# A second up group of each feed-forward as seven block products, and the weave ratio at 0.68

## The chip, the cores and the metric

One core of one Trainium2 chip. The metric is device time in microseconds (us); three runs of the kernel before gave a median of 2243.52 us, from 2241.81 to 2245.09. The profiled execution took 2241.73 us, of which 2240.0 us are the span from the first to the last instruction.

## The reference

One decoder layer in float32 on 256 tokens of width 2048: a SwiGLU feed-forward, a mixer, and a second feed-forward of the same shape. The mixer is not touched here. Each feed-forward computes

```
h = (silu(x @ w_gate) * (x @ w_up)) @ w_down      # w_gate, w_up: 2048 x 5504; w_down: 5504 x 2048
x = x + 0.5 * rms_norm(h, g)
```

The left factor x has 256 rows, so it is two blocks of 128 tokens. All products are made to nearly float32 accuracy: every operand is split into a high and a low part, and three TensorE products stand for one (high by high, high by low, low by high).

## The kernel before, in words

**Names.** PE is TensorE, ACT ScalarE, DVE VectorE, POOL GpSimd. A weight tile of 128 x 1024 floats (512 KB) is loaded by SP's queue into one of 12 buffers `raw`; ACT copies its high part to `whi` (line 171), and DVE subtracts to get the low part `wlo` (line 172). This pair is called a split below. There are five `whi` and five `wlo` buffers, so ACT can make the split of a tile only when PE is done with the split five places earlier. Each engine carries out its instructions in its queue's order.

**Plain group.** `linear_steps` (line 287) multiplies both token blocks by a strip of weights: for each pair of 128-row slices of the weight one split, and 2 x 2 x 3 = 12 matmuls of 512 columns. A gate or up group of 1024 columns is two such strips with 16 slices each: 192 matmuls and 16 splits. Each batch is 12 matmuls, but the last of a strip is 24 with two splits, first 12 for token block 0, then 12 for block 1.

**Seven products.** `sevens` (line 394) makes a group of 1024 columns as a product of 2 x 2 blocks (two token blocks or column halves by two halves of the inner dimension) with seven block products instead of eight, on sums and differences of blocks. The forms of x are made once per feed-forward (`new_forms`). Each block product p has four units s = 0 to 3; a unit is one split and six matmuls, so a group has 28 units, 168 matmuls, 28 splits. Phase one has products 1 and 2 (8 units). Phase two has products 3, 5, 6, 7 and 4 (20 units), with the weights of 5, 6 and 7 summed by DVE in place in the raw tile (line 403, three a round), and the weight of product 4 completed by POOL: an accumulating DMA (line 459) adds a weight block from memory into the raw tile r[0], after product 6 has read that tile. The order of phase two is set by delays; at its end it is p3 s3, p5 s3, p4 s2, p6 s3, p7 s3, p4 s3. Seven DVE additions (lines 455 to 477) put the products together.

```
def t4(s, r):
    G.dma_start(out=r[0].rearrange("p (k c) -> p k c", c=512), in_=src(1, 0, s), accum_op=ALU.add)
    return r[0]
for p, ps in phase(8 * g + 4, [(3, 0, lambda s, r: r[2]), (5, 1.1, lambda s, r: add(r[0], r[1])),
                               (6, 2.2, lambda s, r: add(r[0], r[2])), (7, 3.3, lambda s, r: add(r[2], r[1])),
                               (4, 6.4, t4)]):
```

**Blocks.** `ffn` (line 593) goes by five blocks of 1024 columns (f = 0, 8, 16, 24, 32 in units of 128) and a rest of 384. The gate of block 0 is plain and runs ahead. The gates of f = 8, 16, 24, 32 and the up group of f = 32 are seven-product groups: five groups, 840 matmuls, called the side. The plain up groups of f = 0, 8, 16, 24 with the down products of those blocks (`down_steps`, 192 matmuls a block), and the rest's gate and up (96 matmuls of 384 columns each), are the main work: 1728 matmuls. The down products of the last block and the rest follow after.

**The weave.** `weave` (line 268) sets the order, and PE runs in it. After each batch of n main matmuls it gives the side n x RATIO of credit, and side units are put out while credit is above zero. Where the main work needs a side group (`yield "gate", f`), the missing units are put out one after another with nothing between.

```
credit += n * ratio
while side is not None and credit > 0:
    n = next(side, None)
```

**Up results.** In a plain up strip, `up` (line 624) multiplies the sum by the silu of the gate on DVE (line 627) for each token block, and the transposes of the result on PE (line 178) come after the next 12 matmuls. `up_seven` (line 664) does the multiplication for a whole group (line 668, four DVE instructions), and its transposes come with the main batch that follows.

Of the kernel before, what the change touches and what calls it, by code (L numbers as in the profile page):

```python
# [33 lines left out]
BIG = 5  # L34
BLOCK = 8
AHEAD = 3
UP_SEVEN = (4,)
RATIO = 0.5


def constants():
# [16 lines left out]
def layer(ctx: ExitStack, tc: tile.TileContext, a, out: bass.AP):  # L58
# [191 lines left out]
    def run_soon():  # L250
        while soon:
            soon.pop(0)()
# [15 lines left out]
    def weave(main, side, done, ratio):  # L268


        credit = 0.0
        for n in main:
            if not isinstance(n, int):
                while n not in done:
                    credit -= next(side)
                continue
# [3 lines that stand above are left out]
                if n is None:  # L280
                    side = None
                else:
                    credit -= n
        for _ in side or ():
            pass
# [307 lines left out]
    def ffn(u, r, first, then, head, wg, wu, wd, gpost, resid, keep, gname, final, unscale=None):  # L593
# [23 lines left out]
        def gate_seven(c, f):  # L617
            for t in range(2):
                for i in range(2):
                    x = c[t][:, i * 512:i * 512 + 512]  # L620
                    S.activation(x, x, AF.Silu, scale=scale(t, 1 if i == 0 else -1))
                sg[f][t] = c[t]
# [41 lines left out]
        def up_seven(c, f):  # L664
            for t in range(2):
                for i in range(2):
                    g = sg[f][t][:, i * 512:i * 512 + 512]
                    V.scalar_tensor_tensor(g, c[t][:, i * 512:i * 512 + 512], scale(t, 1 if i == 0 else -1), g, ALU.mult, ALU.mult)

            def later():  # L670
                for i in (0, 4):
                    hT[f + i] = (slot([P, 4, 2, P], F32R, "hh"), slot([P, 4, 2, P], F32R, "hl"))
                    hh, hl = hT[f + i]
                    for t in range(2):
                        split_T(hh[:, :, t, :], hl[:, :, t, :], sg[f][t][:, i * P:(i + 4) * P], 4)

            soon.append(later)
# [4 lines left out]
        for f in range(BLOCK, last, BLOCK):  # L682
            groups.append((("gate", f), wg, f * P, lambda c, f=f: gate_seven(c, f)))
            if f // BLOCK in UP_SEVEN:
                groups.append((("up", f), wu, f * P, lambda c, f=f: up_seven(c, f)))

        def main():
            for f in range(0, last, BLOCK):
                if f and f // BLOCK in UP_SEVEN:
                    if f < f0:  # L690
                        yield "up", f
                        run_soon()
                else:
                    if f:
                        yield "gate", f
                    yield from up_steps(f)
                if f < f0:
                    yield from down_steps(f)
            yield from linear_steps(lu, Weights(KD, chunks(wg, last, m)), lambda t, ps: gate_plain(t, ps, last))
            yield from linear_steps(lu, Weights(KD, chunks(wu, last, m)), lambda t, ps: up(t, ps[0], last, 0, m))  # L700

        done = set()
        weave(main(), sevens(forms, groups, done), done, RATIO)
        run_soon()
# [521 lines left out]
```

## Time and profile before

| | us |
|---|---|
| median of three runs | 2243.52 |
| profiled execution, whole | 2241.73 |
| its span | 2240.0 |
| PE busy | 2201.4 (98% of the span) |
| DVE busy | 1571.3 (70%) |
| ACT busy | 1223.3 (55%) |
| POOL busy | 138.5 (6%) |

The span is the time between the first and the last instruction. Busy time counts each engine's own instructions; a high share does not say that the engine never waits in a given stretch.

### The profile page before, as it was taken

The numbers are of one execution on the slowest core, as the hardware profiler recorded it, in microseconds if no ns is written. First come the engines' busy times: TensorE is split into PE (matmuls) and PEld (weight loads), VectorE is DVE, ScalarE is ACT, GpSimd is POOL, SyncE is SP. The second block draws the span as 40 slices with busy tenths as digits, with TensorE's granted clock in tenths as the row PEclk, the third lists the DMA queues.
The fourth block names the chain that finished last, engine by engine and source line by source line (L and its number), as shares of the span: only waits on it lengthen the run. The fifth ranks groups of instructions, "written<-read, shape, count | busy, mean of one in ns | idle before, by whom it ended". The sixth has DMA issues, their size and how long they took to land.

```text
span 2240.0 us, 28549 instructions
## 1 busy us (share of the span) xinstructions
PE 2201.4 (98%) x10434; PEld 1873.4 (84%) x10434; DVE 1571.3 (70%) x1859; ACT 1223.3 (55%) x1560; POOL 138.5 (6%) x177
## 2 busy tenths in 40 slices
PE   8999999999999999999999999999999999999997
PEld 6888888888887799999888888887888888887886
DVE  6787787877776758686655545558777777787866
ACT  7665656565554654545444444456655565655544
POOL 1001001010011000000000000000010010100110
PEclk9999999999999999999999999999999999999999
DMA  8578879797888464456655566755778797988981
GB/s 326 160 246 239 275 219 285 224 278 235 256 231 314 151 209 127 151 156 182 196 182 192 187 197 204 234 190 181 250 237 275 217 289 232 267 249 245 236 300 55
DMA packets 229245, 497.41 MB, mean 222 GB/s; under 512 B 18360, under 2 KB 51344, under 8 KB 229104
## 3 DMA queue, kind: packets, MB, share of 16 engines
q1 hardware_dynamic: 203456, 436.32, 59.0%
q0 software_dynamic: 25472, 59.20, 12.5%
q8 instruction: 81, 1.33, 0.2%
q14 instruction: 60, 0.49, 0.1%
q10 hardware_dynamic: 176, 0.07, 0.0%
HBM read 472.44 MB, written 23.07 MB: 221 GB/s over the span
## 4 chain that ended last, share of the span: by engine, by line
PE 48%; DVE 2%; issue 1%; DMA 1%; ACT 1%; DVEq 0%; POOL 0%; ACTq 0%; POOLq 0%
PE acc L322 13%; PE acc L319 13%; PE acc L320 13%; PE acc L443 3%; PE acc L441 3%; PE acc L442 3%; PE tp L178 1%; DMA raw<-in_ffn_wu_dram 1%; DVE wlo L172 1%; DMA raw<-in_ffn_wd_dram 0%; ACT whi L171 0%; DVE y L568 0%; DVE ym L568 0%; ACT junk L167 0%; ACT uh L189 0%
## 5 line engine op out<-in xcount | busy, mean ns | idle before, releaser
L172 DVE TENSOR_TENSOR wlo<-raw,whi 128x1024 fp32r<-128x1024 f32 (+2 forms) x937 | 1095.5, 1182 | 557.8 <-ACT whi L171 532.0
L171 ACT ACTIVATE whi<-raw 128x1024 fp32r<-128x1024 f32 (+2 forms) x937 | 953.8, 1028 | 786.8 <-PE acc L322 612.6
L319 PE MATMUL acc<-whi,uh 128*128 128x512 f32 (+1 forms) x1620 | 605.5, 374 | 0.0
L320 PE MATMUL acc<-wlo,uh 128*128 128x512 f32 (+1 forms) x1620 | 600.6, 371 | 4.0 <-DVE wlo L172 4.0
L322 PE MATMUL acc<-whi,ul 128*128 128x512 f32 (+1 forms) x1620 | 525.0, 371 | 0.0
L320 PEld LDWEIGHTS acc<-wlo,uh 128*128 128x128 f32 x1620 | 304.9, 188 | 47.1 <-DVE wlo L172 5.7
L319 PEld LDWEIGHTS acc<-whi,uh 128*128 128x128 f32 x1620 | 305.2, 188 | 41.8 <-ACT mv L796 0.3
L322 PEld LDWEIGHTS acc<-whi,ul 128*128 128x128 f32 x1620 | 302.0, 188 | 41.4
L319 PE MATMUL acc<-whi,hh 128*128 128x512 f32 x688 | 268.1, 390 | 0.0
L320 PE MATMUL acc<-wlo,hh 128*128 128x512 f32 x688 | 267.8, 389 | 0.0
L322 PE MATMUL acc<-whi,hl 128*128 128x512 f32 x688 | 259.4, 389 | 0.0
L320 PEld LDWEIGHTS acc<-wlo,hh 128*128 128x128 f32 x688 | 129.2, 188 | 26.8
L319 PEld LDWEIGHTS acc<-whi,hh 128*128 128x128 f32 x688 | 129.2, 188 | 26.8
L322 PEld LDWEIGHTS acc<-whi,hl 128*128 128x128 f32 x688 | 129.1, 188 | 26.8
L403 DVE TENSOR_TENSOR raw<-raw,raw 128x1024 f32<-128x1024 f32 x120 | 146.3, 1219 | 0.3
L441 PE MATMUL acc<-whi,sh 128*128 128x512 f32 x320 | 126.5, 395 | 0.0
L443 PE MATMUL acc<-whi,sl 128*128 128x512 f32 x320 | 125.0, 391 | 0.0
L442 PE MATMUL acc<-wlo,sh 128*128 128x512 f32 x320 | 124.8, 390 | 0.0
L441 PE MATMUL acc<-whi,uh 128*128 128x512 f32 x240 | 95.1, 396 | 3.7 <-ACT whi L171 3.7
L442 PE MATMUL acc<-wlo,uh 128*128 128x512 f32 x240 | 94.2, 393 | 1.2 <-DVE wlo L172 1.2
L443 PE MATMUL acc<-whi,ul 128*128 128x512 f32 x240 | 94.1, 392 | 0.0
L459 POOL DMA_DIRECT2D raw<-in_ffn_wg_dram x32 | 38.8, 1213 | 641.1 <-DVE wlo L172 523.3
(323 smaller groups left out, 1912.0 us busy)
## 6 DMA issues: line engine op xcount, KB each, us to landing
raw<-in_ffn_wg_dram SPq DMA_DIRECT2D x192, 512.0 KB, 5.0
raw<-in_ffn_wd_dram SPq DMA_DIRECT2D x172, 512.0 KB, 6.2
raw<-in_ffn_wu_dram SPq DMA_DIRECT2D x168, 512.0 KB, 5.2
raw<-in_w_gate_dram SPq DMA_DIRECT2D x96, 512.0 KB, 4.4
raw<-in_w_in_dram SPq DMA_DIRECT2D x192, 192.0 KB, 2.7
raw<-in_ffn_wg_dram POOLq DMA_DIRECT2D x32, 512.0 KB, 8.9
ysum<-part POOLq DMA_DIRECT2D x64, 256.0 KB, 6.5
raw<-in_w_o_dram SPq DMA_DIRECT2D x32, 512.0 KB, 4.6
```

The costliest lines, as they stand in the source:

```text
L171: S.activation(hi, src, AF.Copy)
L172: return V.tensor_tensor(lo, src, f32(hi), ALU.subtract)
L178: PE.transpose(p[:, i, :], src[:, i * P:(i + 1) * P], ident)
L319: PE.matmul(ps[t][c], lh, wh[:, sl], start=(k == 0), stop=False)
L320: PE.matmul(ps[t][c], lh, wl[:, sl], start=False, stop=False)
L322: PE.matmul(ps[t][c], ll, wh[:, span[c]], start=False, stop=(k == nk - 1))
L403: V.tensor_tensor(x, x, y, ALU.add)
L441: PE.matmul(bank[p], ah[:, k, :], hi[:, ws], start=(seen[p] == 0), stop=False)
L442: PE.matmul(bank[p], ah[:, k, :], lo[:, ws], start=False, stop=False)
L443: PE.matmul(bank[p], al[:, k, :], hi[:, ws], start=False, stop=(seen[p] == 7))
L459: G.dma_start(out=r[0].rearrange("p (k c) -> p k c", c=512), in_=src(1, 0, s), accum_op=ALU.add)
```

## The change

The up group of f = 16 (block 2 when the first is block 0) joins the side as a sixth seven-product group, between the gates of f = 16 and f = 24. Its plain up strips leave the main work, which now asks for the group itself (`yield "up", 16`) ahead of the down products of that block. The ratio goes from 0.5 to 0.68. Both feed-forwards use the same function, so both change.

```
-UP_SEVEN = (4,)
-RATIO = 0.5
+UP_SEVEN = (2, 4)
+RATIO = 0.68
```

The lines that read the two constants:

```
groups.append((("gate", f), wg, f * P, lambda c, f=f: gate_seven(c, f)))
if f // BLOCK in UP_SEVEN:
    groups.append((("up", f), wu, f * P, lambda c, f=f: up_seven(c, f)))
...
if f and f // BLOCK in UP_SEVEN:
    if f < f0:
        yield "up", f
        run_soon()
...
weave(main(), sevens(forms, groups, done), done, RATIO)
```

## Rows read from the trace of the kernel before

**Rows 1.** Engine share by stretch: both weaves (start:end, length, busy us, clock, DMA share, GB/s).
```profile
116.50:686.70 570.20, 567.92 (x2567) 473.66 (x2565) 433.09 (x400) 322.74 (x349) 53.67 (x60) 1.00 0.84 250
1578.00:2150.80 572.80, 567.99 (x2567) 473.67 (x2565) 435.33 (x401) 324.37 (x349) 53.79 (x60) 1.00 0.84 250
```

**Rows 2.** Timeline of PE, second feed-forward (start, duration, engine, line, instruction, idle before it).
```profile
1788.62 0.39 PE L441 MATMUL acc<-whi,sh 128*128 128x512 f32 x1
...
1791.34 0.39 PE L319 MATMUL acc<-whi,hh 128*128 128x512 f32 x1
...
2145.97 0.33 PE L319 MATMUL acc<-whi,uh 128*128 128x384 f32 x1
...
2147.89 0.34 PE L322 MATMUL acc<-whi,ul 128*128 128x384 f32 x1
```

**Rows 3.** Timeline of DVE, POOL, ACT, DVE and PE at the end of group gate 16.
```profile
1790.40 3.51 DVE L172 TENSOR_TENSOR wlo<-raw,whi 128x1024 fp32r<-128x1024 f32 x3 [0.57 <-ACT whi L171]
...
1793.06 1.20 POOL L459 DMA_DIRECT2D raw<-in_ffn_wg_dram  x1 [2.48 <-DVE wlo L172]
...
1801.74 2.01 ACT L171 ACTIVATE whi<-raw 128x1024 fp32r<-128x1024 f32 x2 [5.01 <-DMA raw<-in_ffn_wg_dram]
...
1802.84 1.23 DVE L172 TENSOR_TENSOR wlo<-raw,whi 128x1024 fp32r<-128x1024 f32 x1 [4.85 <-ACT whi L171]
...
1806.30 0.39 PE L441 MATMUL acc<-whi,uh 128*128 128x512 f32 x1
```

**Rows 4.** Timeline of POOL and ACT: the same at the first and the last such end.
```profile
215.33 1.24 POOL L459 DMA_DIRECT2D raw<-in_ffn_wg_dram  x1 [2.81 <-DVE wlo L172]
...
224.94 2.01 ACT L171 ACTIVATE whi<-raw 128x1024 fp32r<-128x1024 f32 x2 [5.94 <-DMA raw<-in_ffn_wg_dram]
...
2024.23 1.19 POOL L459 DMA_DIRECT2D raw<-in_ffn_wg_dram  x1 [18.80 <-DVE wlo L172]
...
2033.35 2.96 ACT L171 ACTIVATE whi<-raw 128x1024 fp32r<-128x1024 f32 x3 [5.23 <-DMA raw<-in_ffn_wg_dram]
```

**Rows 5.** Line 459 by itself: its accumulating transfers.
```profile
DMA to landing us min/median/max: 5.6/8.9/11.8
```

**Rows 6.** Timeline of PE at the end of the last side group, both feed-forwards.
```profile
686.74 0.50 PE L441 MATMUL acc<-whi,uh 128*128 128x512 f32 x1 [1.13 <-ACT whi L171]
688.00 0.50 PE L442 MATMUL acc<-wlo,uh 128*128 128x512 f32 x1 [0.76 <-DVE wlo L172]
...
2150.82 0.79 PE L441 MATMUL acc<-whi,uh 128*128 128x512 f32 x1 [2.60 <-ACT whi L171]
2152.08 0.79 PE L442 MATMUL acc<-wlo,uh 128*128 128x512 f32 x1 [0.47 <-DVE wlo L172]
```

**Rows 7.** Timeline of PE: stops for an up result, and one outside the weave.
```profile
576.11 0.66 PE L178 MATMUL tp<-ident,sg 128*128 128x128 f32 x4 [1.19 <-DVE sg L627]
...
696.00 1.53 PE L178 MATMUL tp<-ident,sg 128*128 128x128 f32 x12 [1.83 <-DVE sg L668]
...
770.93 0.70 PE L320 MATMUL acc<-wlo,uh 128*128 128x384 f32 x2 [3.51 <-DVE wlo L172]
...
2038.71 0.66 PE L178 MATMUL tp<-ident,sg 128*128 128x128 f32 x4 [2.23 <-DVE sg L627]
```

**Rows 8.** Engine share by stretch of 10 us (the number before the DMA share is the clock).
```profile
770.00:780.00 10.00, 8.87 (x46) 8.16 (x47) 9.79 (x26) 6.78 (x20) 2.16 (x4) 0.83 0.73 236
...
2030.00:2040.00 10.00, 7.77 (x37) 6.20 (x36) 5.56 (x7) 3.67 (x5) 0.00 (x0) 1.00 0.85 278
...
2150.00:2160.00 10.00, 8.71 (x32) 7.69 (x33) 9.20 (x13) 5.82 (x7) 1.59 (x3) 0.66 1.03 415
```

**Rows 9.** Groups of instructions by line (count, busy us, mean ns of one, idle before).
```profile
L172 DVE TENSOR_TENSOR wlo<-raw,whi 128x1024 fp32r<-128x1024 f32 (+2 forms) x937 | 1095.5, 1182 | 557.8 <-ACT whi L171 532.0
L171 ACT ACTIVATE whi<-raw 128x1024 fp32r<-128x1024 f32 (+2 forms) x937 | 953.8, 1028 | 786.8 <-PE acc L322 612.6
...
L403 DVE TENSOR_TENSOR raw<-raw,raw 128x1024 f32<-128x1024 f32 x120 | 146.3, 1219 | 0.3
...
L474 DVE TENSOR_TENSOR sg<-sg,acc 128x512 f32<-128x512 f32 x10 | 6.8, 680 | 0.0
```

## The prediction

> **What bounds the kernel now.** I read the engine shares over the two weaves first, then PE's timeline for the places where it stops, then the other engines just ahead of each stop. In each weave PE is busy 568 of 570 to 573 us [rows 1], so there every matmul costs its full distance to the next: twelve of 512 columns take 1791.34 - 1788.62 = 2.72 us, 0.227 us each; eleven steps of 384 columns take 1.92 us, 0.174 each [rows 2]. DVE is busy 433 us (76%) and ACT 323 (57%) [rows 1]. So the bound is PE, and the question is where PE will stop.
>
> The place that matters is the end of each side group. The last product-4 unit (p4 s3) needs a raw tile that POOL's accumulating transfer completes, and that transfer can only start when p6 s3, two side units earlier, has been split. At the end of gate 16 it goes out at 1793.06, ACT gets the tile at 1801.74 after 5.01 us of idling, the low half is there at 1802.84 + 1.23 = 1804.07, and PE wants it one matmul after 1806.30 [rows 3]: 2.5 us to spare. All later splits stand behind that one on ACT and DVE meanwhile. Of the eight ends of gate groups seven show this wait on ACT, with 8.1 to 9.9 us (mean 9.1) from issue to ACT's start; the first has 9.6 and the last 9.1 [rows 4].
>
> **The time PE must cover.** With five split buffers, p6 s3 can be split once PE has left the split five places before it. From there to p4 s3 PE has a fixed number of matmuls to run, counted from the loops. Before, the four gate groups of each feed-forward all end with 72 matmuls in that stretch, 72 x 0.227 = 16.3 us. At gate 16 the unit five places earlier is the one whose first matmul is the 1788.62 row [rows 2], so it ends 1.36 us later, at 1789.98. The need is thus 3.1 us to POOL's issue, 9.1 us on the way, and 1.06 + 1.2 us minus one matmul (2.0) for the two halves: 14.2 us, 13.3 to 15.0 by the shortest and longest way. It fits into 16.3.
>
> **The change, part by part (both feed-forwards alike).**
>
> *Matmuls removed.* 192 plain matmuls become 168: 24 fewer, 48 in the kernel, 48 x 0.227 = -10.9 us. The Trainium skill (TensorE: Matmul & The Clock Gate, "Wait — 56ns, not 53.3ns?") gives 215.7 ns for 512 columns at the full clock; by it this term would be -10.4 us; the row says 0.227, and I keep that.
>
> *Work added elsewhere.* 12 more splits (DVE 1.18 us, ACT 1.03), 12 additions of 1.22 and seven of 0.68 [rows 9]: DVE +14.2 + 14.6 + 4.8 = 33.6 us, so (433 + 34)/565 = 83% of the weave; ACT +12 and a copy, 60%. The up product's own DVE work and 16 transposes stay the same in number. Taken at nothing, because PE's matmuls cover it: the heaviest mix (phase two beside a plain up strip) keeps DVE at about 90%. If the cover fails, the price is rival 3. POOL issues four more accumulating transfers and SP four more loads (20 for 16), 4.2 MB per weave on about 143 MB (250 GB/s x 570 us), share 0.84 to about 0.87: nothing, unless the accumulates land later, which the upper end of the need holds. POOL's new transfers stand in its queue among the writes of block 8's down sums, each waiting for an ACT copy; a transfer of up 16 caught behind one has 2.1 us to spare there (16.3 against 14.2). The new loads stand in SP's queue among those of the main strips, which now come 12% slower (one batch and its credit: 20.2 matmuls against 18).
>
> *Ends of groups moved.* This is what the ratio does. At 0.5 one batch of 12 is followed by one unit; at 0.68 by one or two, so there is less main work between p6 s3 and p4 s3. Counting the loops again with six groups at 0.68 gives, for the same stretch:
> - gate 8: 54 matmuls, 12.2 us; short of 14.2 by 2.0 (1.1 to 2.8)
> - gate 16: 60, 13.6 us; short by 0.6 (0 to 1.4)
> - up 16: 72, 16.3 us; nothing
> - gate 24: 48, 10.9 us; short by 3.3 (2.4 to 4.1; nothing with the shortest row of line 459, rival 1). The main work reaches `yield "gate", 24` with 960 x 0.68 = 653 of the 672 matmuls it needs, so the last four units are put out back to back
> - gate 32: 78, 17.7 us; nothing
> - up 32, in the rest: before 24 x 0.227 + 48 x 0.174 = 13.8 us, and PE stopped there: 1.13 + 0.76 us of waits in the first and 2.60 + 0.47 in the second [rows 6]. Now 24 and 36: 11.7 us, so +2.1 on top of that stop.
>
> Sum: 2.0 + 0.6 + 3.3 + 2.1 = 8.0 per feed-forward, +16.0. A wait of PE is lost for good, since PE bounds both sides of it.
>
> *New place: the transposes of up 16.* Between the last matmul of up 16 and its transposes PE has 6 + 12 = 18 matmuls (4.1 us); ahead of them DVE has one addition and four multiplications, some splits between. The nearest row is the same step for up 32, 1.83 us of waiting [rows 7]; from none to 1.8, I take 1.0: +2.0 for both.
>
> *Stops that go.* Before, gate 32 ends in the last batch of a plain up strip, where DVE, held at the late tile, keeps the up multiplication waiting: 1.19 and 2.23 us [rows 7]. Now it ends in a down strip with 17.7 us. With the empty queue behind each, -3.7 us. What is late next there: nothing that these rows show.
>
> *The clock.* A stop of 2.60 us was followed by a stretch at 0.66 of full clock, one of 3.51 by 0.83; one of 2.23 kept 1.00 [rows 6 to 8], the levels being 2.4 and 1.2 GHz. At the lower level 10 us lost 3.4 and 1.7 us of full clock. The stop at gate 24 (two parts, about 2.3 and 1) lies at that border, that of up 32 in the first feed-forward (now about 3.2) beyond it. Zero to three drops; I take the middle, 1.5 x 2.55 = +3.8.
>
> Sum: -10.9 - 3.7 + 16.0 + 2.0 + 3.8 = +7.2. On the profiled 2241.73 us that is 2248.9. This execution lies 1.8 us below the median of 2243.52, against which the change will be timed: 2250.7 us.
>
> **Rivals.**
> 1. *The tile comes in time: faster.* If the transfer lands in 5.6 us, the shortest of line 459 [rows 5], the need falls from 14.2 to 10.7 us, under all gate groups' cover; it decides at about 7 us for gate 8 and 5.7 for gate 24. Left: -10.9 - 3.7 + 4.2 (up 32) + 2.0 = -8.4, 2235 us. For: the shortest row. Against: seven ends at 8.1 or more with DMA at 0.84. The compiler may also hoist p6 s3's split ahead of a main one, with the same effect. On the page's side: the Trainium skill (DMA: Bandwidth & Descriptors, "Anatomy of one DMA — SWDGE (gpsimd) path") fits 2.0 us plus the bytes at 436 GB/s, an estimate of 3.2 us for 512 KB, by which no end would stop and this case would hold; the median of 8.9 speaks against it.
> 2. *No change.* The stops at gate 8 and gate 24 come out at their lower bounds, with no clock drop: 2 x (1.1 + 0 + 2.4 + 2.1) + 2.0 - 14.6 = -1.4, or +1.2 with one drop of 2.55: 2242 to 2245. For: gate 16's transfer reached ACT after 8.7 us [rows 3]. Against: the mean of the seven is 9.1.
> 3. *DVE becomes the bound.* At 83% on average and 90% in places, each of the six plain up strips per feed-forward may hold its transposes like the one of 1.19 us [rows 7]: 12 x 1.2 = 14 us more than the forecast, 2264. Against: with DVE at 98% from 770 to 780 [rows 8] there is only one such row outside the weave, and inside it the two stops of rows 7 both follow a late tile.
>
> **How the numbers follow.** Forecast 0.5, own range 2245 to 2257; rival 1 0.2, rival 2 0.2, rival 3 0.1. About 0.2% (4.5 us) is what a measurement can tell from no change. Faster, under 2239: rival 1 and a little of rival 2, 0.24. Within: most of rival 2 and the low edge of the forecast, 0.22. Slower: 0.54. The range leaves out the far part of rivals 1 and 3: 2235 to 2263.
>
> **What would show it.** Right: PE waits for ACT `whi` at the end of gate 8 (about 1 us for the high half) and of gate 24 (2 us or more) in both feed-forwards, just behind a wait of ACT for line 459's transfer; the stops at the transposes ahead of gate 32's end gone; that of up 32 longer by 2 us; a clock below 1.00 after gate 24. Wrong: no PE wait at gate 24 (rival 1), or waits spread over the up strips' transposes (rival 3). The matmul count must fall by 48, else the change does not do what it says.

## The result and the profile after

The changed kernel takes 2263.45 us (median of 4 runs, 2262.62 to 2268.49) against 2243.81 for the kernel before on the same chip (2241.81 to 2245.09): ratio 1.0093, 95% interval 1.0076 to 1.0111. Slower, as forecast, but by 19.6 us where 7.2 had been worked out, and 0.45 us above the range.

The two weaves carry all of it. From the first matmul of line 441 to the first of the closing down products, PE's timeline gives 587.42 and 590.25 us before, 597.53 and 601.58 after: +10.1 and +11.3. Between the weaves it is 874.1 before and 874.0 after. The 24 matmuls less are in these figures (-5.4 us each), so waits and slow clock grew by 15.6 and 16.8 us per weave. Engine share by stretch of the same two stretches as in [rows 1], after:

```profile
115.90:695.20 579.30, 566.34 (x2531) 468.98 (x2529) 459.74 (x430) 331.99 (x361) 57.05 (x60) 0.99 0.85 253
1587.40:2170.60 583.20, 567.63 (x2533) 469.45 (x2531) 461.73 (x431) 333.90 (x361) 58.12 (x62) 0.99 0.85 251
```

DVE (third busy time) is at 79%, ACT at 57%: on average nothing but PE is near its limit. The timeline of PE at the ends of gate 8, gate 24 and up 32, first and then second feed-forward, shows where it stops (in brackets the wait and who ended it); the pairs from 695.25 and from 2170.60 answer to [rows 6]:

```profile
209.02 0.49 PE L441 MATMUL acc<-whi,uh 128*128 128x512 f32 x1 [2.02 <-ACT whi L171]
210.27 0.80 PE L442 MATMUL acc<-wlo,uh 128*128 128x512 f32 x1 [0.76 <-DVE wlo L172]
...
498.99 0.50 PE L441 MATMUL acc<-whi,uh 128*128 128x512 f32 x1 [3.67 <-ACT whi L171]
500.25 0.77 PE L442 MATMUL acc<-wlo,uh 128*128 128x512 f32 x1 [0.76 <-DVE wlo L172]
...
695.25 0.80 PE L441 MATMUL acc<-whi,uh 128*128 128x512 f32 x1 [3.04 <-ACT whi L171]
696.51 0.80 PE L442 MATMUL acc<-wlo,uh 128*128 128x512 f32 x1 [0.46 <-DVE wlo L172]
...
1680.62 0.50 PE L441 MATMUL acc<-whi,uh 128*128 128x512 f32 x1 [2.66 <-ACT whi L171]
1681.88 0.79 PE L442 MATMUL acc<-wlo,uh 128*128 128x512 f32 x1 [0.76 <-DVE wlo L172]
...
1975.33 0.80 PE L441 MATMUL acc<-whi,uh 128*128 128x512 f32 x1 [5.40 <-ACT whi L171]
1976.59 0.80 PE L442 MATMUL acc<-wlo,uh 128*128 128x512 f32 x1 [0.46 <-DVE wlo L172]
...
2170.60 0.50 PE L441 MATMUL acc<-whi,uh 128*128 128x512 f32 x1 [1.72 <-ACT whi L171]
2171.86 0.50 PE L442 MATMUL acc<-wlo,uh 128*128 128x512 f32 x1 [0.76 <-DVE wlo L172]
```

The clock falls at each of them. The stretches of 10 us below 0.99 in the second weave (number before the DMA share; before, there was only the 0.66 of [rows 8]):

```profile
1680.00:1690.00 10.00, 8.63 (x31) 6.79 (x32) 9.20 (x11) 8.87 (x12) 1.19 (x2) 0.83 0.73 243
...
1970.00:1980.00 10.00, 4.21 (x9) 3.03 (x10) 4.69 (x6) 5.72 (x6) 0.00 (x0) 0.74 0.65 163
1980.00:1990.00 10.00, 10.00 (x42) 8.14 (x42) 9.29 (x10) 5.21 (x7) 0.00 (x0) 0.92 0.86 275
...
2170.00:2180.00 10.00, 8.12 (x34) 7.23 (x34) 9.39 (x13) 6.31 (x8) 2.10 (x4) 0.83 1.03 414
```

Here 1.7 + 2.6 + 0.8 + 1.7 = 6.8 us of full clock are lost, as many in the first weave (0.83, 0.83, 0.74, 0.92): 13.6 in all, against 3.4 before.

The transfer itself did not get slower. Line 459 by itself, after (before: [rows 5]):

```profile
DMA to landing us min/median/max: 5.5/8.9/10.9
```

What is late is its issue. Timelines of POOL, ACT and DVE ahead of the stop at 1975.33 (gate 24), to be read beside [rows 3]:

```profile
1962.70 0.90 POOL L655 DMA_DIRECT2D ysum<-part  x1 [12.43 <-ACT part L650]
1963.75 1.21 POOL L459 DMA_DIRECT2D raw<-in_ffn_wg_dram  x1
...
1958.87 1.06 ACT L171 ACTIVATE whi<-raw 128x1024 fp32r<-128x1024 f32 x1 [1.39 <-DMA raw<-in_ffn_wg_dram]
1960.11 1.06 ACT L171 ACTIVATE whi<-raw 128x1024 fp32r<-128x1024 f32 x1 [0.18 <-DVE raw L403]
...
1974.22 3.90 ACT L171 ACTIVATE whi<-raw 128x1024 fp32r<-128x1024 f32 x4 [9.10 <-DMA raw<-in_ffn_wg_dram]
...
1957.51 1.23 DVE L172 TENSOR_TENSOR wlo<-raw,whi 128x1024 fp32r<-128x1024 f32 x1 [1.54 <-ACT whi L171]
1958.77 1.22 DVE L403 TENSOR_TENSOR raw<-raw,raw 128x1024 f32<-128x1024 f32 x1
1959.96 1.22 DVE L172 TENSOR_TENSOR wlo<-raw,whi 128x1024 fp32r<-128x1024 f32 x1
1961.10 1.22 DVE L403 TENSOR_TENSOR raw<-raw,raw 128x1024 f32<-128x1024 f32 x1
1962.24 1.22 DVE L172 TENSOR_TENSOR wlo<-raw,whi 128x1024 fp32r<-128x1024 f32 x1
```

Here DVE works without a gap from 1957.51 to 1963.46. The split of p6 s3 on ACT (1960.11) had to wait for its addition (1958.77), and its low half (1962.24) stands behind the next product's addition (1961.10). POOL issues at 1963.75. The split buffer was free at 1958.88, when the 1.36 us unit starting with the first line-441 matmul at 1957.53 ended: 4.9 us from buffer to issue (called the lag below), where [rows 3] had 3.1. POOL issues 0.29 us after the end of that low half, so the write just ahead of it in POOL's queue (1962.70) did not hold it up. The rows for gate 8, gate 24, gate 8 and gate 24, in order of time (the first matmul of the unit five places earlier, whose buffer is free 1.36 us later, and POOL's issue):

```profile
193.21 0.40 PE L441 MATMUL acc<-whi,sh 128*128 128x512 f32 x1
198.85 1.19 POOL L459 DMA_DIRECT2D raw<-in_ffn_wg_dram  x1 [16.00 <-DVE wlo L172]
...
482.92 0.39 PE L441 MATMUL acc<-whi,sh 128*128 128x512 f32 x1
489.09 1.21 POOL L459 DMA_DIRECT2D raw<-in_ffn_wg_dram  x1
...
1664.18 0.40 PE L441 MATMUL acc<-whi,sh 128*128 128x512 f32 x1
1671.43 1.19 POOL L459 DMA_DIRECT2D raw<-in_ffn_wg_dram  x1 [17.97 <-issue]
...
1957.53 0.39 PE L441 MATMUL acc<-whi,sh 128*128 128x512 f32 x1
```

That is 4.3, 4.8, 5.9 and 4.9 us. In the third, POOL issues only 1.07 us after the low half's end; what held it for the last 0.8 us is not shown. The lag grew behind larger covers too, where no stop shows it: 3.8 us at up 16, 4.6 and 4.9 at gate 32.

The lateness is also seen in who made ACT wait over the whole run (total us, times, longest), first before, then after:

```profile
ACT whi L171 <- DMA raw<-in_ffn_wg_dram: 40.7, 10, 6.2
...
ACT whi L171 <- DVE raw L403: 7.8, 8, 2.6
```

```profile
ACT whi L171 <- DMA raw<-in_ffn_wg_dram: 86.4, 23, 9.9
ACT whi L171 <- DVE raw L403: 71.7, 44, 3.7
```

### The profile page after: what moved, and what is told of

The parts are those of the page before. It is cut to its first block, busy times and chain, and to the rows that moved or that the text cites. A ratio compares the mean times of both kernels' runs of the same rounds, so it can differ in the third digit from the quotient of the medians.

```text
span 2261.8 us, 28631 instructions
## 1 busy us (share of the span) xinstructions
PE 2203.8 (97%) x10386; PEld 1869.0 (83%) x10386; DVE 1625.8 (72%) x1921; ACT 1243.4 (55%) x1586; POOL 149.3 (7%) x185
## 4 chain that ended last, share of the span: by engine, by line
PE 26%; issue 20%; DVE 2%; DMA 2%; POOL 2%; ACT 1%; POOLq 0%; DVEq 0%; ACTq 0%
PE acc L322 8%; PE acc L320 8%; PE acc L319 8%; DMA raw<-in_ffn_wg_dram 2%; DVE wlo L172 1%; POOL raw L459 1%; POOL ysum L655 1%; PE tp L178 0%; DMA raw<-in_ffn_wu_dram 0%; ACT whi L171 0%; DVE y L568 0%; POOL ysum L653 0%; PE acc L442 0%; PE acc L443 0%; DMA raw<-in_ffn_wd_dram 0%
## 5 line engine op out<-in xcount | busy, mean ns | idle before, releaser
L320 PE MATMUL acc<-wlo,uh 128*128 128x512 f32 (+1 forms) x1492 | 551.9, 370 | 6.0 <-DVE wlo L172 6.0
L319 PE MATMUL acc<-whi,uh 128*128 128x512 f32 (+1 forms) x1492 | 556.4, 374 | 0.0
L322 PE MATMUL acc<-whi,ul 128*128 128x512 f32 (+1 forms) x1492 | 475.6, 370 | 0.0
L319 PEld LDWEIGHTS acc<-whi,uh 128*128 128x128 f32 x1492 | 281.8, 189 | 37.0 <-ACT mv L796 0.3
L322 PEld LDWEIGHTS acc<-whi,ul 128*128 128x128 f32 x1492 | 278.4, 189 | 36.2
L403 DVE TENSOR_TENSOR raw<-raw,raw 128x1024 f32<-128x1024 f32 x144 | 175.5, 1219 | 1.0
L441 PE MATMUL acc<-whi,sh 128*128 128x512 f32 x384 | 150.8, 393 | 0.0
L443 PE MATMUL acc<-whi,sl 128*128 128x512 f32 x384 | 149.9, 390 | 0.0
L442 PE MATMUL acc<-wlo,sh 128*128 128x512 f32 x384 | 149.7, 390 | 0.0
L441 PE MATMUL acc<-whi,uh 128*128 128x512 f32 x288 | 116.2, 403 | 18.5 <-ACT whi L171 18.5
L443 PEld LDWEIGHTS acc<-whi,sl 128*128 128x128 f32 x384 | 72.1, 188 | 15.3
```

What stands on the lines that cost most here:

```text
L319: PE.matmul(ps[t][c], lh, wh[:, sl], start=(k == 0), stop=False)
L320: PE.matmul(ps[t][c], lh, wl[:, sl], start=False, stop=False)
L322: PE.matmul(ps[t][c], ll, wh[:, span[c]], start=False, stop=(k == nk - 1))
L403: V.tensor_tensor(x, x, y, ALU.add)
L441: PE.matmul(bank[p], ah[:, k, :], hi[:, ws], start=(seen[p] == 0), stop=False)
L442: PE.matmul(bank[p], ah[:, k, :], lo[:, ws], start=False, stop=False)
```

## The experiments

Times are medians; ratios are to the kernel before, run on the same chip, with 95% intervals.

**The transfer as the sole cause, in both kernels.** After, without line 459's transfer:

```
-                G.dma_start(out=r[0].rearrange("p (k c) -> p k c", c=512), in_=src(1, 0, s), accum_op=ALU.add)
                 return r[0]
```

> The changed kernel without the accumulating transfer of product 4, which so has only part of its weights (that part of the computation is left out). Theory (late tile): nothing waits for the tile any more; no PE stop at a group's end, no clock drop in a weave: 2228 to 2238 us, the saving of 10.9 us and the old stops too. Rival (added work of the sixth group): DVE's and ACT's instructions are the same in number, so 2255 us or more.

2213.29 us, 0.9869 [0.9854, 0.9883], 15 us below the expected range. The kernel before with the same edit:

> The kernel before without line 459's accumulating transfer (one block of product 4's weights is left out). It is the partner of the changed kernel without it (2213.3). Theory (the matmul term is whole, 48 x 0.227 = 10.9 us, and everything that turned it into a loss stands on that transfer): 2222.5 to 2226, that is 9 to 13 us above the partner, with both weaves within 1 to 3 us of matmul pace. Rival (part of the matmul gain is lost elsewhere: transposes, VectorE, more loads): less than 6 us above the partner, under 2219.

2224.71 us, 0.9915 [0.9901, 0.9928], as the theory said. Engine share of both weaves, kernel before without the transfer:

```profile
116.00:700.00 584.00, 583.68 (x2660) 488.80 (x2659) 454.88 (x427) 336.12 (x363) 30.36 (x42) 1.00 0.78 238
1575.00:2150.00 575.00, 575.00 (x2618) 481.66 (x2618) 449.40 (x419) 332.28 (x357) 30.36 (x42) 1.00 0.78 238
```

And the changed kernel without it:

```profile
116.00:700.00 584.00, 583.68 (x2661) 489.06 (x2660) 484.66 (x460) 349.88 (x378) 30.36 (x42) 1.00 0.79 245
1575.00:2150.00 575.00, 574.62 (x2621) 481.52 (x2620) 477.19 (x452) 345.07 (x371) 30.35 (x42) 1.00 0.79 246
```

PE (first busy time) is never more than 0.4 us short of the stretch and the clock is 1.00. The two differ by 11.4 us; 48 matmuls at 0.227 are 10.9. So the matmul term is whole, and the transfer costs 18.5 us before and 50 after: the change adds 31.7 us of stops and slow clock on it. All of DVE's new work is still there in the 2213 us kernel; its amount is not the cause.

**The ratio alone, on the kernel before.**

```
-RATIO = 0.5
+RATIO = 0.68
```

> The kernel before with the ratio at 0.68 and nothing else: no sixth seven-product group, 48 more matmuls than the changed kernel. Theory (late tile): the ratio alone decides how much work PE has at the end of each side group. Counted from the loops the five ends now have 12.2, 13.6, 16.3, 10.9 and 19.0 us of matmuls (before: four times 16.3, then 13.8). PE stops of about 3 us at gate 8 and 4 to 6 us at gate 32 with clock drops behind them; the stop at up 32 goes. Time 2248 to 2262 us. Rival (the sixth group's added work on DVE and the queues is what costs): no sixth group, so 2240 to 2247 us.

2251.25 us, 1.0036 [1.0023, 1.0049]: slower with no work added. Gate 8 stops (2.84 and 1.50 us at its last unit), with 5.4 and 5.1 us from buffer to issue, and line 403 makes ACT wait 64.8 us in 35 waits, from 7.8 in 8. So pairs of units bring DVE's additions ahead of the splits without a sixth group; at gate 8 the cover is the 12.2 us of the changed kernel too. The stop of 4 to 6 us expected at gate 32 did not come at its last unit (PE waited 2.68 us at transposes just ahead of it in the first feed-forward).

**Another ratio, on the changed kernel** (0.68 to 0.70 in the same line).

> The changed kernel with the ratio at 0.70 for 0.68: the same work in another order. Theory (late tile): the six ends have 16.3 us five times and 13.8 us at up 32, as the ends of the kernel before have, so the stops at gate 8 and gate 24 and the clock drops behind them go, and the 10.9 us of matmuls saved come through: 2231 to 2239 us. Rival (the sixth group's added work costs): the side is denser still, so 2258 us or more.

2245.28 us, 1.0008 [0.9998, 1.0018], 18 us less from a step of 0.02: neither range held it. By the count of the loops the cover is then 72 matmuls, 16.3 us, at every end but the last (13.8), and of the stops at gates 8 and 24 one wait of 0.53 us is left; besides, PE stops at up 16 (0.82 and 0.85 us), for low halves soon after it (1.61 and 1.74), and at transposes for DVE (the longest 2.21 and 3.19). The buffer-to-issue time at up 16 is 8.9 and 9.1 us there, with ACT waiting 105.6 us for line 403: cover alone does not decide it.

**The clock by itself.** Idle matmuls ahead of the last unit of gates 8 and 24:

```
+                if p == 4 and s == 3 and first // 8 in (0, 3):
+                    idle = acc(512)
+                    for _ in range(10 if first < 8 else 16):
+                        PE.matmul(idle, ah[:, 0, :], ah[:, :4, :].rearrange("p k c -> p (k c)"), start=True, stop=True)
```

> The changed kernel with 10 matmuls of 512 columns, whose result nobody uses, put before the last product-4 unit of gate 8, and 16 before that of gate 24, in both feed-forwards: 52 matmuls, 11.8 us at full pace, all in places where PE waited 2.8 to 5.9 us. Theory (late tile, with the clock as the larger part): the waits get shorter by what the matmuls fill, no clock drop follows there, and the time falls by 5 to 8 us to 2255 to 2259 us although PE does more. Rival (the drops of the clock cost next to nothing, the wait is the cost): 2262 to 2267 us.

2263.1 us, 1.0095 [1.008, 1.011]; missed. The clock stays at 1.00 around both gates and half of the 13.6 lost us is back, but the time is the same. The 52 idle matmuls take 11.8 us, PE's waits at lines 441 and 442 fall by about 10, and later ends stop longer. Counted from the starts of matmuls, the slow stretches cost 6.3 us less, while the ends of gate 16 and up 32 stop 4.4 us longer, with transfers there of 9.5 to 11.8 us from issue to ACT's start (7.9 to 11.0 without the idle matmuls). That gives back most of the gain; why those transfers took longer is not settled.

**Product 4 later** (order p6 s3, p7 s3, p4 s2, p4 s3, so p4 s2 no longer stands ahead of p6 s3): changed kernel, kernel before, and changed kernel at 0.70.

```
-                                           (4, 6.4, t4)]):
+                                           (4, 8.4, t4)]):
```

> The changed kernel with product 4 later in phase two (delay 8.4 for 6.4): its unit s comes after p7 of round s + 1, so the end of a group reads p6 s3, p7 s3, p4 s2, p4 s3. Nothing is added or removed. Theory (chain): the accumulates of one group wait for each other, since p4 s2 stood ahead of p6 s3 on ACT and DVE; now it stands behind, and PE has 17.7, 16.3, 17.7, 12.2, 23.1 and 14.5 us of matmuls at the six ends. Only gate 24 and up 32 can still stop, by 2 us each: 2218 to 2232 us. Rival (the wait is in the DVE queue, filled by the sixth group's additions, whatever the order): 2255 us or more.

> The kernel before with product 4 later in phase two (delay 8.4 for 6.4), five groups, ratio 0.5. Theory (chain): the ends have 17.7 us three times, 20.4 and 15.2 us of matmuls; the stops that the kernel before had at gate 32 and up 32 (7.8 us and 10.5 us of lost pace in the two feed-forwards) mostly go: 2227 to 2237 us. Rival: unchanged within 4 us.

> Six groups, ratio 0.70, delay 8.4: the ends have 17.7 us five times and 15.2 us at up 32. Theory (chain): as without any accumulate, but for a short stop at up 32: 2213 to 2222 us, below both kernels. Rival (DVE's added work): 2240 us or more, as at 0.70 with the old order.

2234.1 us, 0.9961 [0.9946, 0.9976]; 2229.93, 0.9941 [0.9926, 0.9956]; 2227.95, 0.9928 [0.9911, 0.9944]. More cover (gate 8 17.7 for 12.2 us, gate 24 12.2 for 10.9) takes 29 us off the changed kernel and 14 off the one before. The direction held; the first and the third came out 2 and 6 us above the expected range, with stops of 1.44 and 1.88 us left at gate 24 in the first, where buffer to issue still takes 5.2 us. So p4 s2's place is not what makes the issue late at gate 24. The kernel at 0.70 with this order is faster than both kernels of the comparison.

**Only the last round's transfer** (changed kernel; product 4's weights of the other rounds lack a block).

```
+                if s == 3:
                     G.dma_start(out=r[0].rearrange("p (k c) -> p k c", c=512), in_=src(1, 0, s), accum_op=ALU.add)
```

> The changed kernel, in which product 4 takes its accumulating transfer in the last of the four rounds only (product 4 lacks part of its weights in the other three, so that part of the computation is left out). The order of all instructions on PE, ACT and DVE is meant to stay. Theory (chain): the last transfer now goes out about 3.1 us after its buffers are free, as in the kernel before, so the ends need 14.2 us again and stop by what the prediction had for them (2.0 at gate 8, 3.3 at gate 24, 2.5 to 4 at up 32, some clock): 2238 to 2252 us. Rival (ends are late by themselves): 2257 us or more.

2255.94 us, 1.0054 [1.004, 1.0069]: between the two. Buffer to issue falls to 3.6 us at gate 8, but stays 4.8 at gate 24, where PE waits 4.4 and 4.2 us for the high half. The earlier rounds' transfers are part of the lateness at gate 8 and none of it at gate 24.

**DVE's additions taken away** (changed kernel).

```
 def add(x, y):
-    with tc.issue_after(weight_splits[-AHEAD].ins):
-        V.tensor_tensor(x, x, y, ALU.add)
     return x
```

> The changed kernel without the three in-place additions of phase two (12 a group), so the weights of products 5, 6, 7 and 4 are wrong in part; 88 us of VectorE work are gone in each feed-forward (72 additions of 1.22 us). Theory (a round of phase two costs VectorE 5 x 1.18 + 3 x 1.22 = 9.6 us against 30 x 0.227 = 6.8 us of matmuls, so where units come back to back the low halves fall behind, and line 459's transfer goes out 4.3 to 5.9 us after its split buffer is free instead of 3.1): that lag falls to about 3 us at gates 8 and 24, the stop at gate 24 from 3.8 and 5.6 us to 2.5 to 3.5, that at gate 8 to 1 or less, and with some clock the time falls to 2246 to 2256. Rival (the lag comes from the accumulating transfer of the round before, or from the split buffers alone): 2260 to 2266, lag unchanged. The transfer itself stays, so nothing near the 2213 of the kernel without it is expected.

2229.41 us, 0.9935 [0.992, 0.9951], 17 us below the expected range. The lag fell as the theory said: buffer to issue is 2.8 to 3.6 us at gates 8 and 24. Timelines of POOL, ACT and DVE at gate 24, second feed-forward, the same place as above:

```profile
1939.44 1.21 POOL L457 DMA_DIRECT2D raw<-in_ffn_wg_dram  x1 [11.91 <-DVE wlo L172]
...
1936.82 1.06 ACT L171 ACTIVATE whi<-raw 128x1024 fp32r<-128x1024 f32 x1 [0.30 <-PE acc L441]
...
1945.32 4.85 ACT L171 ACTIVATE whi<-raw 128x1024 fp32r<-128x1024 f32 x5 [2.46 <-DMA raw<-in_ffn_wg_dram]
...
1935.19 3.95 DVE L172 TENSOR_TENSOR wlo<-raw,whi 128x1024 fp32r<-128x1024 f32 x3 [1.49 <-ACT whi L171]
...
1946.41 3.50 DVE L172 TENSOR_TENSOR wlo<-raw,whi 128x1024 fp32r<-128x1024 f32 x3 [3.19 <-ACT whi L171]
```

ACT makes p6 s3's split (1936.82) as soon as PE has left the buffer (it waited for PE, not for DVE), the low halves of three splits follow one another, the last of them p6 s3's, and POOL issues 0.30 us after it (1935.19 + 3.95 = 1939.14). ACT starts on the completed tile 5.9 us later, and PE does not stop. The order and the cover are those of the changed kernel. But the lag is not the only thing that changed: at gates 8 and 24 the four transfers took 5.9 to 8.1 us from issue to ACT's start (mean 6.7), where the changed kernel's took 8.1 to 10.5 (mean 9.1). On average the lag is 1.9 us shorter and the way 2.4; by the prediction's sum, a lag of 3.1 us with a way of 9.1 leaves PE stops of 2.0 and 3.3 us at these ends. So this run shows that the additions make the issue late, but how much of the 34 us that they cost goes through the issue and how much through slower transfers is not separated. What remains is the tail, the end of up 32 (3.05 and 2.87 us), whose buffer-to-issue time is 2.8 us, as in the changed kernel (2.9).

**The transfer replaced: SP loads the block into a raw tile of its own, DVE adds it.** First at 0.68, then at 0.70.

```
-            for blocks in (((0, 0), (1, 0)), ((0, 0), (0, 1), (1, 1))):
+            for blocks in (((0, 0), (1, 0)), ((0, 0), (0, 1), (1, 1), (1, 0))):
...
-                G.dma_start(out=r[0].rearrange("p (k c) -> p k c", c=512), in_=src(1, 0, s), accum_op=ALU.add)
-                return r[0]
+                return add(r[0], r[3])
```

> The changed kernel with product 4's last block loaded by SP into a raw tile of its own, ahead of time, and added by VectorE (line 403's addition) in place of POOL's accumulating transfer: 24 additions of 1.22 us more for VectorE in each feed-forward (29 us, some 88% of the weave), the 9 us on the way gone from the end of each group. Theory (all stops of the weave hang on that transfer): the need falls from 14 to 17 us to 4 + 1.2 + 2 = 7, under the smallest cover (10.9); both weaves come within 1.5 to 6 us of matmul pace, 2213 to 2226. Rival (VectorE, or the 12 raw buffers that now hold four tiles a round, become the bound): 2235 or more, with stops spread over transposes and splits.

> The plain load and addition as before, with the ratio at 0.70. Theory: with the transfer gone the ratio has nothing to set, so it stands within 4 us of the same kernel at 0.68 (2211 to 2226), where the accumulating kernels lay 18 us apart (2263 and 2245). Rival (the ratio sets how VectorE's work is bunched, transfer or not): more than 8 us apart.

2222.97 us, 0.991 [0.9896, 0.9923], the fastest complete version here, 40 us under the changed kernel; and 2239.43, 0.9982 [0.9974, 0.9991]. The first held. The second fell to its rival, 16 us apart: how units bunch matters without the transfer too. DVE and then PE at the end of up 16 in the second kernel:

```profile
397.46 1.22 DVE L172 TENSOR_TENSOR wlo<-raw,whi 128x1024 fp32r<-128x1024 f32 x1
398.59 0.68 DVE L471 TENSOR_TENSOR sg<-sg,acc 128x512 f32<-128x512 f32 x1
399.19 1.22 DVE L172 TENSOR_TENSOR wlo<-raw,whi 128x1024 fp32r<-128x1024 f32 x1
400.33 0.68 DVE L667 SCALAR_TENSOR_TENSOR sg<-sg,sg 128x512 f32<-128x512 f32 x1
400.93 0.68 DVE L473 TENSOR_TENSOR sg<-sg,acc 128x512 f32<-128x512 f32 x1
401.53 0.68 DVE L474 TENSOR_TENSOR sg<-sg,acc 128x512 f32<-128x512 f32 x1
402.13 0.68 DVE L667 SCALAR_TENSOR_TENSOR sg<-sg,sg 128x512 f32<-128x512 f32 x1
402.73 0.68 DVE L476 TENSOR_TENSOR sg<-sg,acc 128x512 f32<-128x512 f32 x1
403.33 1.22 DVE L172 TENSOR_TENSOR wlo<-raw,whi 128x1024 fp32r<-128x1024 f32 x1
...
404.60 0.50 PE L442 MATMUL acc<-wlo,uh 128*128 128x512 f32 x1 [1.18 <-DVE wlo L172]
```

DVE has no gap for these 7 us, and here PE waits for it directly. ACT's waits for line 403 are 174.2 us there, 115.1 at 0.68. That this bunching makes up the whole 16 us was not tested apart.

## Why the prediction was right in sign and wrong in size

- *Matmuls removed, -10.9*: right; 11.4 between the two kernels without the transfer.
- *On the way, 9.1 us*: right. From POOL's issue to ACT's start the twelve ends after have 6.9 to 11.0 us, mean 9.1.
- *Cover per end*: right where it could be seen. Gates 8 and 24 stop, gate 16, up 16 and gate 32 have no stop over 0.5 us at the last unit's first matmul.
- *The need of 14.2 us*: **this step failed, by its term of 3.1 us to POOL's issue.** I read it at the ends of before and carried it over to ends where units follow one another. It measured 4.3 and 5.9 us at gate 8 and 4.8 and 4.9 at gate 24, so the need there is 15.4 to 17.0 by that alone. Counted from the starts of matmuls (a stop costs 0.4 to 0.7 us more than its two brackets say, as 1.25 us from 209.02 to 210.27 less 0.227 is 1.02 where the bracket has 0.76), gate 8 stops for 3.2 and 3.8 us and gate 24 for 4.9 and 6.6: 18.5 in all, forecast 2 x (2.0 + 3.3) = 10.6. The four lags exceed 3.1 by 7.4 us in all and the four ways average 9.1, so the lag is nearly the whole of the 7.9 us missed there.
- *Gate 16, 0.6 each*: buffer to issue was 3.1 us there, as taken. In the first feed-forward nothing came, the way being 7.9 us; in the second it was 9.1, and 0.9 us came, at the transposes ahead of the last unit and at its low half. *The tail, +2.1 each*: too large. By the brackets the waits are 3.50 and 2.48 us, 1.89 and 3.07 before [rows 6]: +1.0 for both. The cover fell as counted, but buffer to issue fell too, from 3.6 and 3.7 us to 2.9, and in the second feed-forward the way was 9.7 us for 11.9 before, which no part of the sum had foreseen.
- *Work added on DVE, at nothing*: the same error at its root. On average it holds (79%). But one round of phase two is 5 x 1.18 + 3 x 1.22 = 9.6 us of DVE [rows 9] beside 30 x 0.227 = 6.8 us of matmuls. Alone among main batches a unit is covered (3.1 us in [rows 3]); in pairs or back to back DVE falls behind just ahead of the one split that starts the transfer, as the rows from 1957.51 to 1963.75 show. Without the additions the time fell by 34 us (in part because the transfers landed sooner), without the transfer by 50: the additions cost this much only because a transfer hangs on them.
- *The clock, +3.8*: too small, 13.6 - 3.4 = +10.2 in the profile. In part of that slow time PE stood still anyway: from the starts of its matmuls the slow stretches cost 11.3 us after and 2.4 before, +8.9. The idle matmuls show that even this does not come back whole when the drops go.
- *Transposes of up 16, +1.0 each*: 0.47 and 0.54 us. *Stops that go, -3.7*: right, no such row is left; at the plain strips' transposes PE waits 0.8 us in the whole run, against 6.3 before.

Of the 14.6 us by which the profiled runs differ from the forecast (2263.55 - 2241.73 = 21.8, less 7.2), gates 8 and 24 are +7.9, the clock +5.1, gate 16 -0.3 and the tail -3.2. The other 5.1 are smaller waits spread over the weaves. The largest are five of PE for a low half on DVE, which the prediction had at nothing: 0.98 and 1.22 us in the up strip after gate 16, 1.49 in the down strips after up 16 of the second feed-forward, 0.66 twice at the second unit of up 32. They were not traced one by one.

Rival 3 named nearly the time that came, 2264, but not its place, the plain strips' transposes. Rivals 1 and 2 needed the low bound of the need; it went above the high one (15.0).

## What to carry to other kernels

A lead time read from a profile holds only for the spacing in which it was read: before work is moved closer together, count each engine's busy time over the few units around the critical transfer, not over the stage. A long transfer whose start hangs on work of the moment makes a schedule brittle (0.68 to 0.70 moved 18 us); loading the operand ahead and paying 1.2 us of DVE for the addition brought more than any ratio or order tried with the transfer in place, though DVE then stands at 87% of the weave, and the 16 us between its two ratios suggest that its own bunching decides next.

## What the runs showed of the chip

- Two waits close together, 2.66 and 0.76 us at gate 8, were followed by a granted clock of 0.83 over the next 10 us, which is 3.4 us at the lower of the two levels; the single wait of 2.23 us in [rows 7] left it at 1.00 [rows 8]. The length of a stop alone does not tell: with product 4 later, waits of 1.44 and 0.76 us at gate 24 of the first feed-forward kept 1.00, and 1.18 and 0.76 at up 32 of the second were followed by 3.4 us at the lower level.
- Without DVE's additions the accumulating transfers landed sooner, 7.9 us median against 8.9, with the same sizes and a DMA share no lower (0.88 for 0.85). Whether the additions themselves or the times of issue make the difference was not tried.
